# The affine maps of four layer norms moved from GpSimd to VectorE, in pieces between the stages that follow

## The chip, the cores and the metric

One Trainium2 chip; the kernel runs on 1 core. The metric is the time of one execution in microseconds (us). Engines are named as the profile names them: PE is TensorE's matmul stream, PEld its weight loads, DVE VectorE, ACT ScalarE, POOL GpSimd, SP the queue that issues most of the transfers. A line number such as L868 is a line of the kernel before.

## What is computed

The reference has two blocks of depth two on 512 tokens of width 1024 in 32-bit floats. The change lies in the second block, whose loop is:

```python
for l in range(DEPTH):
    mix = even_mixer(x, ...) if l % 2 == 0 else odd_mixer(x, ...)
    x = layer_norm(ALPHA * x + mix, ln1_g[l], ln1_b[l])
    hdn = jnp.square(jax.nn.relu(x @ ffn_w1[l]))
    x = layer_norm(ALPHA * x + hdn @ ffn_w2[l], ln2_g[l], ln2_b[l])
    e = rms_norm(p[l] @ ple_w_proj[l], ple_norm_g[l])
    x = x + jax.nn.sigmoid(x @ ple_w_gate[l]) * e
```

with `layer_norm(x, g, b) = (x - mean) * rsqrt(var + eps) * g + b`. So there are four layer norms, and each result is used twice: as the input of the next matrix product, and as the residual `x` to which that stage's result is added.

## The kernel before, in words

**Data.** The residual `x` lies in SBUF as 4 token tiles of 128 x 1024. Every matrix product runs at raised precision: each operand is split into a high part (rounded by a cast on ACT) and a low part (the rest, by a subtraction on DVE), and three matmuls go into the same PSUM tile (`mm3`, L140 to L142). A weight chunk of 512 KB is loaded by SP into `wraw` (3 buffers, L133), cast on ACT (`whi`, L134) and subtracted on DVE (`wlo`, L135). Activations are split in the same way (`Thi`, L291; `spt`, L293 or L295; `Tlo`, L296).

**Layer norm** (`layer_norm`, L844 to L861). For a pair of token tiles DVE computes the statistics (`bst` L854, `bmv` L855, `brs` L856 and L857), ACT the square root (L858), and DVE writes the normalised value over `x` (L859). PE transposes `x` (`psT`, L273), and the affine map for the matmul operand is applied after the transposition, when the tiles are split, with columns of gain and bias (L291 to L296). The residual needs the same map on `x` itself. That is `ln_affine`: POOL loads gain and bias as rows (`gr`, `br`, L821; one buffer each, used again by the next layer norm) and then, token tile by token tile, multiplies `x` by `gr` (L868) and adds `br` (L869), 128 x 1024 each. A tile's map can begin only when PE has transposed it.

**After ln1: the opening of the feed-forward stage.** `ple_e` (PE `pse`, ACT copies L920, squares L924, roots L927, DVE L925 to L928) is traced before it and runs beside ln1's second pair. Then `mlp` goes over 8 blocks of 512 hidden units. For a unit group `f`, `rows(f, o)` does 24 matmuls into `psu`, and then ACT takes the relu (`r`, L332), POOL squares it (`q`, L333), ACT rounds it (`uh`, L334) and DVE subtracts (`ul`, L335). In the first block, alone, the rows are cut in two halves of 256 tokens: f = 0, 1, 2 for the first half, f = 0, 1, 2 for the second, then f = 3 for both. After a block's rows come the matmuls with W2 into `psy`; the result is added to `x` on DVE (L877 the first time, L879 later), and that is where the mapped `x` is needed first.

**After ln2: the gate** (`ple_gate`). `proj_out` computes the gate's left 512 columns for the 4 token tiles (4 weight chunks, `psj`), then the right 512 columns (4 chunks with buffers of their own). Each result goes through `ev`: ACT takes the sigmoid (`pg`, L939), DVE multiplies by `e` (L940) and adds to `x` (L941). In layer 0 the next layer's activations are made from each finished tile (`pso`, L634; `Tlo`, L639); in layer 1 each finished tile is written out.

**Order.** Each engine works through its own queue in order. The queues are laid out when the kernel is built, from the order of the source and from when an instruction can start by an estimate; so an instruction that stands later in the source is put ahead where an earlier one isn't ready. `issue_after(i)` only adds that what is issued inside it stands behind `i` on `i`'s engine.

Of the kernel before, what the change touches and what calls it, by code (L numbers as in the profile page):

```python
# [18 lines left out]
P = 128  # L19
D = 1024  # L20
KT = D // P
# [57 lines left out]
def each(gen):  # L79
    return lambda t: next(gen, None)  # L80


def pairs(gen):
    return lambda t: t % 2 and next(gen, None)


class Net:
# [72 lines left out]

    def proj_out(self, acts, W, pp, rp, toks, evac, after, mid=None):
        hi, lo = acts
        self.proj_tok(acts, W[:, :512], pp, toks, lambda t, ps: evac(t, slice(0, 512), ps), mid)
        ps_of = lambda t: pp.tile([P, 512], F32, name="psj", tag="ps")[:, :256]
        if rp is None:
            for c0 in (512, 768):
                sl = slice(c0, c0 + 256)
                for t in self.proj_cols(acts, W[:, sl], ps_of, toks, lambda t, ps: evac(t, sl, ps)):  # L170
                    if c0 == 768:
                        after(t)
            return
        ws = [self.wsplit(W[c * 256:(c + 1) * 256, 512:].rearrange("(k p) n -> p k n", p=P), 2, 512, rp, f"w{c}") for c in range(KT // 2)]
        for t in toks:
            ps = pp.tile([P, 512], F32, name="psj", tag="ps")
            s = slice(t * P, (t + 1) * P)
            for k in range(KT):
                wh, wl = ws[k // 2]
                self.mm3(ps, hi[k][:, s], lo[k][:, s], wh[:, k % 2, :], wl[:, k % 2, :], k == 0, k == KT - 1)  # L180
            evac(t, slice(512, D), ps)
            after(t)
# [118 lines left out]

    def mlp(self, acts, W1, W2, T, st_name, add, ada=None, after=None):
        nc = self.nc
        hi, lo = acts
        toks = range(T // P)
        with ExitStack() as st:
            up = self.pool(st, st_name + "u", 2)
            tp = self.pool(st, st_name + "t", 2)  # L310
            by_pair = T <= 512
            lp = self.pool(st, st_name + "l", 1) if by_pair else None
            pu = self.pool(st, st_name + "pu", 3 if T > 512 else 2, PSUM)
            py = self.pool(st, st_name + "py", 2 if T > 512 else 4, PSUM)
            bg = iter(())
            if ada is not None:
                bg = self.ada_in(ada, (0,), self.pool(st, st_name + "pa", 1, PSUM), self.pool(st, st_name + "ra", 1))
            for fb in range(8):
                st_ = 256 if fb == 0 else 512
                us, ws = [], []  # L320
                for f in range(4):
                    us.append([up.tile([P, T], F32R, name="u" + n, tag=f"u{n}{f}") for n in "hl"])

                def rows(f, o):
                    w = min(st_, T - o)
                    (wh, wl), (uh, ul) = ws[f], us[f]
                    ps = pu.tile([P, 512], F32, name="psu", tag="psu")[:, :w]
                    for k in range(KT):
                        self.mm3(ps, wh[:, k, :], wl[:, k, :], hi[k][:, o:o + w], lo[k][:, o:o + w], k == 0, k == KT - 1)
                    r = tp.tile([P, 512], F32, name="r", tag="r")  # L330
                    q = tp.tile([P, 512], F32, name="q", tag="q")
                    nc.scalar.activation(r[:, :w], ps, AF.Relu)  # L332
                    nc.gpsimd.tensor_tensor(q[:, :w], r[:, :w], r[:, :w], MUL)  # L333
                    nc.scalar.copy(uh[:, o:o + w], q[:, :w])  # L334
                    nc.vector.tensor_tensor(ul[:, o:o + w], q[:, :w], uh[:, o:o + w].bitcast(F32), SUB)  # L335


                for fs in (range(3), range(3, 4)) if fb == 0 else ([f] for f in range(4)):
                    for f in fs:
                        fc = fb * 4 + f  # L340
                        ws.append(self.wsplit(W1[:, fc * P:(fc + 1) * P].rearrange("(k p) n -> p k n", p=P), KT, P))
                    for o in range(0, T, st_):
                        for f in fs:
                            rows(f, o)
                    for f in fs:
                        next(bg, None)
                last = fb == 7
                ws = {}
                for pr in ([toks[i:i + 2] for i in range(0, len(toks), 2)] if last and by_pair else [toks]):
                    for hf in range(2):  # L350
                        if hf not in ws:
                            ws[hf] = [self.wsplit(W2[(fb * 4 + 2 * c) * P:(fb * 4 + 2 * c + 2) * P, hf * 512:(hf + 1) * 512]
                                                  .rearrange("(k p) n -> p k n", p=P), 2, 512, *((lp, f"l{c}") if last and hf and by_pair else ())) for c in range(2)]

                        steps = [(t, range(4)) for t in pr]
                        if by_pair and hf == 0 and pr[0] == 0:
                            steps[:2] = [(t, fs) for fs in (range(3), range(3, 4)) for t in pr[:2]]
                        pss = {}
                        for t, fs in steps:
                            if t not in pss:  # L360
                                pss[t] = py.tile([P, 512], F32, name="psy", tag="psy")
                            ps, s = pss[t], slice(t * P, (t + 1) * P)
                            for f in fs:
                                wh, wl = ws[hf][f // 2]
                                self.mm3(ps, us[f][0][:, s], us[f][1][:, s], wh[:, f % 2, :], wl[:, f % 2, :], f == 0, f == 3)
                            if fs[-1] < 3:
                                continue
                            add(t, hf, ps, last)
                            if last and hf and after is not None:
                                after(t)  # L370
            for _ in bg:
                pass
# [445 lines left out]
class Net2(Net):  # L818
# [45 lines left out]
    def ln_affine(self, x, nm, layer, tp):  # L864
        gr = self.bcast_row(tp, self.A[nm + "_g_2"][layer], D, "gr")
        br = self.bcast_row(tp, self.A[nm + "_b_2"][layer], D, "br")
        for t in range(NX):
            self.nc.gpsimd.tensor_tensor(x[:, t, :], x[:, t, :], gr, MUL)  # L868
            self.nc.gpsimd.tensor_tensor(x[:, t, :], x[:, t, :], br, ADD)  # L869

    def res_add(self, x, first):
        nc = self.nc
# [16 lines left out]
            return f  # L889
        return first  # L890

    def ffn(self, x, acts, layer, after):
        self.mlp(acts, self.A["ffn_w1_2"][layer], self.A["ffn_w2_2"][layer], SX, f"f{layer}", self.res_add(x, self.firsts()), after=after)


    def ple_e(self, pool, layer):
# [31 lines left out]
                nc.vector.scalar_tensor_tensor(e[:, t, :], in0=e[:, t, :], scalar=ss, in1=gr, op0=MUL, op1=MUL)  # L928
        return e

    def ple_gate(self, x, acts, e, layer, after):
        nc, A = self.nc, self.A
        with ExitStack() as s:
            tp = self.pool(s, "plgt", 1)
            pp = self.pool(s, "plgps", 6, PSUM)

            def ev(t, c, ps):
                g = tp.tile([P, 512], F32, name="pg", tag="pg", bufs=3)
                nc.scalar.activation(g, ps, AF.Sigmoid)  # L939
                nc.vector.tensor_tensor(g, g, e[:, t, c], MUL)  # L940
                nc.vector.tensor_tensor(x[:, t, c], x[:, t, c], g, ADD)  # L941
            self.proj_out(acts, A["ple_w_gate_2"][layer], pp, tp, list(range(NX)), ev, after)


    def rope16(self, z, t, nh, cosp, sinp, tp):
# [443 lines left out]
    def second(self, x, acts, Tp, done):  # L1389
        with ExitStack() as s0:  # L1390
# [3 lines left out]
            for layer in range(2):  # L1394
# [14 lines left out]
                s = ExitStack()  # L1409
                ep = self.pool(s, "ep", 1)  # L1410
                e = self.ple_e(ep, layer)
                self.ln_affine(x, "ln1", layer, ep)
                nacts = self.act_tiles(Yp, SX)
                ln2 = self.layer_norm(x, "ln2", layer, nacts, lp)
                self.ffn(x, acts, layer, pairs(ln2))
                drain(ln2)
                self.ln_affine(x, "ln2", layer, ep)
                if layer == 0:
                    Xp = self.pool(s0, "U2", 1, side="right")
                    acts = self.act_tiles(Xp, SX)  # L1420
                    xa = self.x_acts(x, acts)
                    self.ple_gate(x, nacts, e, layer, each(xa))
                    drain(xa)
                else:
                    self.ple_gate(x, nacts, e, layer, done)
                s.close()
                self.dbg(f"l{layer}", x)

# [64 lines left out]
class Net3(Net2):  # L1493
# [832 lines left out]
    def first(self, st):  # L2326
        self.prologue()
        x, xc = self.layer0(self.rwkv_norm)
        self.dbg0(x, xc)
        return self.layer1(x, st)  # L2330
# [43 lines left out]
```

## Time and profile before

| | us |
|---|---|
| median of 3 runs | 3755.2 (3750.63 to 3758.21) |
| the profiled execution | 3759.0 |
| its span in the profile | 3757.2 |
| PE busy in it | 3554.0 |
| DVE busy | 2065.8 |
| ACT busy | 1531.4 |
| POOL busy | 726.0 |

The span is the part of the execution that the profile shows; 1.8 us lie around it. The four places of the change are called here by what they are: the opening of layer 0 (from about 2584 us of the span to 2645), the first gate (2955 to 3033), the opening of layer 1 (3296 to 3366) and the last gate (3681 to the end). A row with a bracket at its end gives the idle time of the engine before that instruction and what ended it. Busy times of engines overlap and don't add up to the span.

### The profile page before, as it was taken

How to read it: one execution, taken by the hardware profiler on the slowest of the kernel's cores; microseconds unless marked ns; L12 is line 12 of the kernel's file. 1: busy time of each engine (PE TensorE's matmuls, PEld its weight loads, DVE VectorE, ACT ScalarE, POOL GpSimd, SP SyncE). 2: the span in 40 equal slices, each digit the busy share in tenths (PEclk: the TensorE clock that was granted, in tenths of full speed). 3: DMA queues.
4: the chain of work that ended last, by engine and by line, in shares of the span. 5: the costliest groups of instructions: out<-in, count | busy, mean ns of one | idle time of the engine just before them, and what ended most of it. 6: DMA issues, size and time to landing. Idle time of an engine off the chain costs nothing.

```text
span 3757.2 us, 63564 instructions
## 1 busy us (share of the span) xinstructions
PE 3554.0 (95%) x26108; PEld 2920.4 (78%) x26108; DVE 2065.8 (55%) x3937; ACT 1531.4 (41%) x2956; POOL 726.0 (19%) x588
## 2 busy tenths in 40 slices
PE   7999999999989988889799999998999899989998
PEld 5767877888865657777588889988888799978886
DVE  5556433333457778899454345567444744573346
ACT  5556332222234655556442234354222345442233
POOL 2100033433222010001224440003111200031112
PEclk9999999999989998888899999999999999989999
DMA  5132233222222782322433332122333321223332
GB/s 182 61 103 95 68 99 104 64 65 62 73 88 71 277 298 91 92 80 87 157 118 95 96 95 91 57 63 87 103 97 90 96 64 60 78 79 100 97 95 68
DMA packets 308211, 370.80 MB, mean 99 GB/s; under 512 B 31712, under 2 KB 228304, under 8 KB 305872
## 3 DMA queue, kind: packets, MB, share of 16 engines
q1 hardware_dynamic: 298752, 340.28, 28.7%
q0 software_dynamic: 8912, 26.39, 2.2%
q8 instruction: 205, 3.36, 0.4%
q14 instruction: 86, 0.70, 0.1%
q10 hardware_dynamic: 256, 0.07, 0.0%
HBM read 324.71 MB, written 41.98 MB: 98 GB/s over the span
## 4 chain that ended last, share of the span: by engine, by line
PE 53%; DVE 9%; ACT 2%; issue 2%; DMA 1%; POOL 0%; SPq 0%; DVEq 0%; ACTq 0%; POOLq 0%
PE psu L142 5%; PE psu L141 5%; PE psu L140 5%; PE psy L142 5%; PE psy L140 4%; PE psy L141 4%; PE psj L140 4%; PE psj L142 4%; PE psj L141 4%; DVE T L2078 1%; DVE Tlo L296 1%; DVE pr L2077 1%; PE S L972 1%; PE psk L140 1%; PE psk L141 1%
## 5 line engine op out<-in xcount | busy, mean ns | idle before, releaser
L135 DVE TENSOR_TENSOR wlo<-wraw,whi 128x1024 fp32r<-128x1024 f32 (+1 forms) x402 | 505.3, 1259 | 543.1 <-ACT whi L134 542.4
L134 ACT CAST whi<-wraw 128x1024 fp32r<-128x1024 f32 (+1 forms) x402 | 417.1, 1039 | 920.2 <-PE psy L142 528.2
L140 PE MATMUL psu<-Thi,whi 128*128 128x512 f32 (+1 forms) x1408 | 499.9, 355 | 8.7 <-ACT r L332 6.0
L142 PE MATMUL psu<-Thi,wlo 128*128 128x512 f32 (+1 forms) x1408 | 501.1, 356 | 0.3 <-DVE wlo L135 0.3
L141 PE MATMUL psu<-Tlo,whi 128*128 128x512 f32 (+1 forms) x1408 | 499.6, 355 | 0.0
L140 PE MATMUL psj<-whi,Thi 128*128 128x256 f32 (+1 forms) x1568 | 482.9, 310 | 10.4 <-ACT whi L134 7.6
L142 PE MATMUL psj<-whi,Tlo 128*128 128x256 f32 (+1 forms) x1568 | 473.8, 303 | 2.5 <-DVE Tlo L296 2.5
L141 PE MATMUL psj<-wlo,Thi 128*128 128x256 f32 (+1 forms) x1568 | 474.3, 303 | 1.2 <-DVE wlo L135 1.0
L140 PE MATMUL psy<-whi,uh 128*128 128x512 f32 x1152 | 452.7, 393 | 3.3 <-ACT whi L134 2.0
L142 PE MATMUL psy<-whi,ul 128*128 128x512 f32 x1152 | 455.0, 395 | 0.0
L141 PE MATMUL psy<-wlo,uh 128*128 128x512 f32 x1152 | 452.3, 393 | 0.0
L333 POOL TENSOR_TENSOR q<-r 128x512 f32<-128x512 f32 (+1 forms) x176 | 235.3, 1337 | 880.0 <-ACT r L332 880.0
L140 PEld LDWEIGHTS psj<-whi,Thi 128*128 128x128 f32 x1568 | 300.2, 192 | 27.4 <-ACT whi L134 9.5
L142 PEld LDWEIGHTS psj<-whi,Tlo 128*128 128x128 f32 x1568 | 299.6, 191 | 15.0 <-DVE Tlo L296 4.2
L141 PEld LDWEIGHTS psj<-wlo,Thi 128*128 128x128 f32 x1568 | 300.3, 192 | 13.0 <-DVE wlo L135 2.5
L140 PEld LDWEIGHTS psu<-Thi,whi 128*128 128x128 f32 x1408 | 268.3, 191 | 52.1 <-ACT r L332 8.1
L141 PEld LDWEIGHTS psu<-Tlo,whi 128*128 128x128 f32 x1408 | 268.4, 191 | 40.7
L142 PEld LDWEIGHTS psu<-Thi,wlo 128*128 128x128 f32 x1408 | 268.3, 191 | 38.5 <-DVE wlo L135 0.7
L335 DVE TENSOR_TENSOR ul<-q,uh 128x512 fp32r<-128x512 f32 (+1 forms) x176 | 105.0, 597 | 316.4 <-ACT uh L334 316.1
L142 PEld LDWEIGHTS psy<-whi,ul 128*128 128x128 f32 x1152 | 216.8, 188 | 53.2 <-DVE ul L335 6.5
L140 PEld LDWEIGHTS psy<-whi,uh 128*128 128x128 f32 x1152 | 216.7, 188 | 52.3 <-ACT whi L134 2.4
L141 PEld LDWEIGHTS psy<-wlo,uh 128*128 128x128 f32 x1152 | 216.9, 188 | 47.2
(545 smaller groups left out, 6100.8 us busy)
## 6 DMA issues: line engine op xcount, KB each, us to landing
wraw<-in_mlp_w_dram SPq DMA_DIRECT2D x128, 512.0 KB, 3.9
wraw<-in_ffn_w_dram SPq DMA_DIRECT2D x128, 512.0 KB, 3.8
wraw<-in_ada_w_dram SPq DMA_DIRECT2D x64, 512.0 KB, 4.8
wraw<-in_ev_w_in_dram SPq DMA_DIRECT2D x28, 512.0 KB, 3.6
scr_bk<-BK SPq DMA_DIRECT2D x16, 768.0 KB, 3.3
wraw<-in_od_w_in_dram SPq DMA_DIRECT2D x24, 512.0 KB, 3.6
BK<-scr_bk SPq DMA_DIRECT2D x14, 768.0 KB, 4.7
wraw<-in_rwkv_w_rkv_dram SPq DMA_DIRECT2D x16, 512.0 KB, 4.6
```

The lines of the kernel that those rows point to most:

```text
L134: nc.scalar.copy(hi, raw)
L135: nc.vector.tensor_tensor(lo, raw, hi.bitcast(F32), SUB)
L140: mm(ps, lhsT=ah, rhs=bh, start=start, stop=False)
L141: mm(ps, lhsT=ah, rhs=bl, start=False, stop=False)
L142: mm(ps, lhsT=al, rhs=bh, start=False, stop=stop)
L296: nc.vector.tensor_tensor(lo[k][:, s], t[:, :w], hi[k][:, s].bitcast(F32), SUB)
L333: nc.gpsimd.tensor_tensor(q[:, :w], r[:, :w], r[:, :w], MUL)
L335: nc.vector.tensor_tensor(ul[:, o:o + w], q[:, :w], uh[:, o:o + w].bitcast(F32), SUB)
L972: nc.tensor.matmul(S[e][:, c], lhsT=q[r], rhs=k[r, c], start=True, stop=True)
L2077: nc.vector.tensor_tensor(pv, T[:, j + 1:, j:j + 1].to_broadcast([P, n, j]), T[:, j:j + 1, 0:j].to_broadcast([P, n, j]), MUL)
L2078: nc.vector.tensor_tensor(T[:, j + 1:, 0:j], T[:, j + 1:, 0:j], pv, ADD)
```

## The change

`ln_affine` still loads the rows `gr` and `br`, but no longer issues the map. It returns a function `affine(t, c)` that multiplies and adds on VectorE, for token tile `t` and columns `c`, behind the last VectorE instruction traced so far. In the feed-forward stage `affine(f)` for whole tiles is called after `rows(f, second half)` for f = 0, 1, 2 and after `rows(3, first half)`, in the first block only. In the gate, the left 512 columns of all four tiles are mapped after the left half's matmuls and before its first evaluation; the right 512 columns of tile 0 after the left half's last evaluation, and of tile t + 1 after the right half's evaluation of tile t. The splitting of the right half's weights (`last_ws`) now stands in the source ahead of the left half's evaluations and behind those four maps.

```diff
-    def proj_out(self, acts, W, pp, rp, toks, evac, after, mid=None):
+    def proj_out(self, acts, W, pp, rp, toks, evac, after, mid=None, between=None):
         hi, lo = acts
-        self.proj_tok(acts, W[:, :512], pp, toks, lambda t, ps: evac(t, slice(0, 512), ps), mid)
+        ws = []
+
+        def last_ws():
+            if rp is not None and not ws:
+                ws.extend(self.wsplit(W[c * 256:(c + 1) * 256, 512:].rearrange("(k p) n -> p k n", p=P), 2, 512, rp, f"w{c}") for c in range(KT // 2))
+
+        def first(t, ps):
+            if between is not None and t == toks[0]:
+                between()
+                last_ws()
+            evac(t, slice(0, 512), ps)
+        self.proj_tok(acts, W[:, :512], pp, toks, first, mid)
...
-        ws = [self.wsplit(W[c * 256:(c + 1) * 256, 512:].rearrange("(k p) n -> p k n", p=P), 2, 512, rp, f"w{c}") for c in range(KT // 2)]
+        last_ws()
...
                     for o in range(0, T, st_):
                         for f in fs:
                             rows(f, o)
+                            if early is not None and fb == 0 and (f == 3) != (o > 0):
+                                early(f)
...
     def ln_affine(self, x, nm, layer, tp):
         gr = self.bcast_row(tp, self.A[nm + "_g_2"][layer], D, "gr")
         br = self.bcast_row(tp, self.A[nm + "_b_2"][layer], D, "br")
-        for t in range(NX):
-            self.nc.gpsimd.tensor_tensor(x[:, t, :], x[:, t, :], gr, MUL)
-            self.nc.gpsimd.tensor_tensor(x[:, t, :], x[:, t, :], br, ADD)
+
+        def affine(t, c=slice(0, D)):
+            with self.tc.issue_after(self.last_of(mybir.EngineType.DVE)):
+                self.nc.vector.tensor_tensor(x[:, t, c], x[:, t, c], gr[:, c], MUL)
+                self.nc.vector.tensor_tensor(x[:, t, c], x[:, t, c], br[:, c], ADD)
+        return affine
+
+    def last_of(self, engine):
+        return next(i for i in reversed(self.nc.cur_bb.bb.instructions) if i.engine == engine)
...
                 nc.scalar.activation(g, ps, AF.Sigmoid)
                 nc.vector.tensor_tensor(g, g, e[:, t, c], MUL)
                 nc.vector.tensor_tensor(x[:, t, c], x[:, t, c], g, ADD)
-            self.proj_out(acts, A["ple_w_gate_2"][layer], pp, tp, list(range(NX)), ev, after)
+                n = t + 1 if c.start else t + 1 - NX
+                if 0 <= n < NX:
+                    affine(n, slice(512, D))
+
+            def mid():
+                for t in range(NX):
+                    affine(t, slice(0, 512))
+            self.proj_out(acts, A["ple_w_gate_2"][layer], pp, tp, list(range(NX)), ev, after, between=mid)
```

The remaining lines hand `affine` from `second` through `ffn` and `ple_gate`.

## Rows read from the trace of the kernel before

**Rows 1.** The page: busy us, share of the span and instructions of each engine.
```profile
PE 3554.0 (95%) x26108; PEld 2920.4 (78%) x26108; DVE 2065.8 (55%) x3937; ACT 1531.4 (41%) x2956; POOL 726.0 (19%) x588
```

**Rows 2.** Groups on POOL, whole span: count | busy us, mean ns | idle before, releaser.
```profile
L868 POOL TENSOR_TENSOR x<-x,gr 128x1024 f32<-128x1024 f32 x16 | 42.5, 2679 | 105.2 <-PE psT L273 102.2 <-DMA gr<-in_ln_g_dram 3.0
```

**Rows 3.** Timeline of POOL, first gate: start us, duration us, engine, line.
```profile
2963.23 5.07 POOL L868 TENSOR_TENSOR x<-x,gr 128x1024 f32<-128x1024 f32 x2 [16.95 <-PE psT L273]
```

**Rows 4.** Timeline of DVE, first gate, the same columns.
```profile
2963.41 2.63 DVE L296 TENSOR_TENSOR Tlo<-spt,Thi 128x256 fp32r<-128x256 f32 x1
...
2984.33 0.43 DVE L296 TENSOR_TENSOR Tlo<-spt,Thi 128x256 fp32r<-128x256 f32 x1
...
3009.38 1.21 DVE L135 TENSOR_TENSOR wlo<-wraw,whi 128x1024 fp32r<-128x1024 f32 x1
...
3010.52 0.68 DVE L940 TENSOR_TENSOR pg<-pg,ple_e 128x512 f32<-128x512 f32 x1
```

**Rows 5.** Groups on DVE, 2963 to 2974 (first gate, pair one on POOL).
```profile
L296 DVE TENSOR_TENSOR Tlo<-spt,Thi 128x256 fp32r<-128x256 f32 x4 | 8.9, 2235 | 0.0
```

**Rows 6.** Groups on DVE, 2586 to 2611 (opening of layer 0).
```profile
L296 DVE TENSOR_TENSOR Tlo<-spt,Thi 128x256 fp32r<-128x256 f32 x8 | 13.4, 1702 | 0.5 <-ACT spt L293 0.4
...
L135 DVE TENSOR_TENSOR wlo<-wraw,whi 128x1024 fp32r<-128x1024 f32 x3 | 5.7, 1894 | 0.0
```

**Rows 7.** Groups on DVE, 3302 to 3335 (opening of layer 1).
```profile
L296 DVE TENSOR_TENSOR Tlo<-spt,Thi 128x256 fp32r<-128x256 f32 x13 | 16.1, 1246 | 1.6 <-ACT spt L293 1.5
...
L135 DVE TENSOR_TENSOR wlo<-wraw,whi 128x1024 fp32r<-128x1024 f32 x3 | 5.9, 1953 | 0.0
```

**Rows 8.** Waits of PE, 2962 to 3003 (first gate): us in total, times, longest.
```profile
PE psT L273 <- DVE bmv L855: 8.2, 1, 8.2
...
PE psj L142 <- DVE Tlo L296: 1.3, 2, 0.8
```

**Rows 9.** Waits of PE, 2588 to 2615 (opening of layer 0).
```profile
PE pse L140 <- DVE pTl L911: 3.1, 1, 3.1
...
PE psu L140 <- ACT ple_e L920: 2.7, 1, 2.7
...
PE pse L140 <- ACT ple_e L920: 0.6, 1, 0.6
```

**Rows 10.** Waits of PE, 3302 to 3341 (opening of layer 1).
```profile
PE psT L273 <- DVE x L859: 5.0, 2, 2.9
...
PE pse L140 <- DVE pTl L911: 3.4, 1, 3.4
...
PE psu L140 <- ACT r L332: 3.2, 1, 3.2
...
PE pse L140 <- ACT ple_e L920: 1.2, 1, 1.2
```

**Rows 11.** PE in four stretches: length, busy (count), granted clock, DMA share, GB/s.
```profile
2614.00:2621.00 7.00, 6.89 (x34) 0.55 0.54 195
2979.00:2986.00 7.00, 6.32 (x20) 0.53 0.58 207
3340.00:3344.00 4.00, 4.00 (x21) 0.57 0.41 131
3705.50:3709.50 4.00, 3.66 (x14) 0.54 0.63 202
```

**Rows 12.** DVE in the opening of layer 0, the same columns.
```profile
2628.00:2644.00 16.00, 7.17 (x10) 1.00 0.44 131
```

**Rows 13.** Timeline of DVE there: [idle us <-releaser].
```profile
2628.89 0.42 DVE L335 TENSOR_TENSOR ul<-q,uh 128x256 fp32r<-128x256 f32 x1 [0.94 <-ACT uh L334]
```

**Rows 14.** PE there, matmuls on W2 alone (tile psy): length, busy (count), granted clock.
```profile
2637.00:2643.00 6.00, 5.91 (x26) 1.00 0.39 111
```

**Rows 15.** Timeline of POOL there.
```profile
2627.06 1.37 POOL L333 TENSOR_TENSOR q<-r 128x256 f32<-128x256 f32 x1 [3.03 <-ACT r L332]
...
2635.46 0.61 POOL L333 TENSOR_TENSOR q<-r 128x256 f32<-128x256 f32 x1 [0.80 <-ACT r L332]
```

More of the change, by code (lines that the diff above doesn't have):

```diff
@@ L300, in act_tiles, with mlp @@
         return tuple(Parts(pool.tile([P, KT, width or T], F32R, name="T" + n, tag=tag + n)[:, :, :T]) for n in ("hi", "lo"))
-    def mlp(self, acts, W1, W2, T, st_name, add, ada=None, after=None):
+    def mlp(self, acts, W1, W2, T, st_name, add, ada=None, after=None, early=None):
         nc = self.nc
@@ L890, in firsts, with ffn @@
         return first
-    def ffn(self, x, acts, layer, after):
-        self.mlp(acts, self.A["ffn_w1_2"][layer], self.A["ffn_w2_2"][layer], SX, f"f{layer}", self.res_add(x, self.firsts()), after=after)
+    def ffn(self, x, acts, layer, after, affine):
+        self.mlp(acts, self.A["ffn_w1_2"][layer], self.A["ffn_w2_2"][layer], SX, f"f{layer}", self.res_add(x, self.firsts()), after=after, early=affine)
     def ple_e(self, pool, layer):
@@ L929, in ple_e, with ple_gate @@
         return e
-    def ple_gate(self, x, acts, e, layer, after):
+    def ple_gate(self, x, acts, e, layer, after, affine):
         nc, A = self.nc, self.A
@@ L1411, in second @@
                 e = self.ple_e(ep, layer)
-                self.ln_affine(x, "ln1", layer, ep)
+                affine = self.ln_affine(x, "ln1", layer, ep)
                 nacts = self.act_tiles(Yp, SX)
                 ln2 = self.layer_norm(x, "ln2", layer, nacts, lp)
-                self.ffn(x, acts, layer, pairs(ln2))
+                self.ffn(x, acts, layer, pairs(ln2), affine)
                 drain(ln2)
-                self.ln_affine(x, "ln2", layer, ep)
+                affine = self.ln_affine(x, "ln2", layer, ep)
                 if layer == 0:
@@ L1421, in second @@
                     xa = self.x_acts(x, acts)
-                    self.ple_gate(x, nacts, e, layer, each(xa))
+                    self.ple_gate(x, nacts, e, layer, each(xa), affine)
                     drain(xa)
                 else:
-                    self.ple_gate(x, nacts, e, layer, done)
+                    self.ple_gate(x, nacts, e, layer, done, affine)
                 s.close()
```

## The prediction, made before the changed kernel was run

> **What bounds the kernel now.** I read the page first, then the groups of the lines that the change takes out, then the four places where they run: POOL's and DVE's timelines side by side, PE's waits there, and the granted clock behind the longest waits. PE is busy for 95% of the span [rows 1], so over the whole kernel it is the bound, and only time in which PE stands still, or runs at the lower clock because it stood still, can be won. The map's two lines hold POOL for 16 multiplications of 2.68 us [rows 2] and 16 additions of about the same, and no engine is shown waiting for their results. What matters is what they do to DVE. While POOL multiplies [rows 3], DVE's subtraction of one `Tlo` tile takes 2.63 us; the same shape takes 0.43 us when POOL is idle [rows 4]. The 2.63 ends when POOL's instruction of about 2.5 us (two in 5.07) ends: the two engines don't share the time, one stands until the other has finished. Subtractions of two SBUF tensors are hit in this way wherever a map runs.
>
> The Trainium skill says the same in SBUF — State Buffer, section "Who interferes with whom": a VectorE instruction with two SBUF inputs contends with a GpSimd instruction that reads SBUF, and whichever issues first holds the pair of ports for the whole instruction. The rows agree. By that rule the change turns the block around, which is the third rival below.
>
> How long DVE stood so: in the first gate, four `Tlo` took 8.9 us instead of 4 x 0.43, so 7.2 [rows 5]. In layer 0's opening eight took 13.4 (10.0 too much) and three `wlo` 5.7 instead of 3 x 1.21 (2.1) [rows 4, 6]. In layer 1's opening thirteen took 16.1 (10.5) and three `wlo` 5.9 (2.3) [rows 7]. PE's waits at the same places are for DVE, or for an ACT that waits in its queue for DVE: 8.2 and 1.3 in the first gate [rows 8]; 3.1, 2.7 and 0.6 in layer 0's opening [rows 9]; 5.0, 3.4, 3.2 and 1.2 in layer 1's [rows 10]. The last gate repeats the first within 0.1 us in each wait, so it is costed by the first gate's rows. Behind the waits PE ran at the lower of its two levels, 1.2 instead of 2.4 GHz, for most of each stretch: 0.55, 0.53, 0.57 and 0.54 granted [rows 11].
>
> **What goes.** The 32 POOL instructions. *First gate*: the 8.2 us wait is for the norm of the second pair, which stands in DVE's queue behind those four `Tlo`; without 7.2 it is 1.0. The 1.3 comes from the second pair's map, and goes. The stretch at 0.53 had 6.32 us busy [rows 11], of which 0.47, 3.0 us, was lost; a wait of 1.0 should not bring it. 7.2 + 1.3 + 3.0 = 11.5. *Last gate*: the same with a shorter low stretch, 3.66 x 0.46 = 1.7, so 10.2. *Layer 0's opening*: of the first 3.1 only 2.1 is the stretched `wlo` (the rest is the transposition of the second pair); 2.7 and 0.6 are for ACT, which waited for the roots behind DVE. 5.4, and 6.89 x 0.45 = 3.1 of clock: 8.5. *Layer 1's opening*: 12.8 of waits against 12.8 of stretching. I take 10 of it, since the norm's own steps keep part of the first two waits, and 4.00 x 0.43 = 1.7 of clock: 11.7. In all 41.9.
>
> **What comes.** A DVE subtraction of 128 x 1024 takes 1.21 us and a product of 128 x 512 in SBUF 0.68 [rows 4]; the maps are of these shapes and both inputs lie in SBUF. An opening gets 8 x 1.21 = 9.7 us, a gate 16 x 0.68 = 10.9, over both layers 41.2, about as much as goes. What of it lies on the path?
>
> In an opening they stand between `ul` of the second half, which begins at 2628.89 [rows 13], and the first additions to `x`. In 2628 to 2644 DVE is busy for 7.17 of 16 us [rows 12], so 8.8 is free for 9.7. Behind the maps in DVE's queue stand the four later `ul` and two `wlo` of W2's first chunks: from 2629.3, 9.7 + 4 x 0.43 + 2 x 1.21 ends at 2643.1. PE begins with W2 at 2637.1, 26 matmuls in 5.91 us, so 0.23 each [rows 14], and wants the second chunk after 6 of them, at 2638.5. It would be 4.6 late, against 18 matmuls (4.1 us) on the first chunk that the other three token tiles offer, if the queue of PE is laid out so. Bounds: 0, and 4.6 with 3.1 of low clock, 7.7. I take 2 for each opening, near the low end, because that cover is almost as long as the delay. POOL's queue loses its only long work; the next `gr` and `br` loads, which reuse the buffers, wait there for the last map, and a `q` behind them for up to one map (2.4 us), beside rows that PE has already done. SP's queue keeps its order; the right half's weight loads are moved ahead of the evaluations in the source only.
>
> In a gate the left maps (8 x 0.68 = 5.4) lie where DVE, rid of the stretching, has room; they can stand ahead of a `Tlo` or a `wlo` one at a time. The right maps stand behind an evaluation each and ahead of the next, where PE needs 24 matmuls of 0.23, 5.5 us, for a tile and DVE 4 x 0.68 = 2.7; in layer 0 they can hold up a `Tlo` of the next layer by 1.4, which that pace hides. The last evaluation has no map behind it, so the tail is as before. Bounds 0 and 5.4; I take 1 for each gate, one or two maps, as only one at a time can slip in.
>
> **The sum.** 41.9 - 2 x 2 - 2 x 1 = 35.9 less. Against the profiled execution, 3759.0, that is 3723.1; the median of the runs shown is 3.8 lower, and for it I predict 3755.2 - 35.9 = 3719.
>
> **Rivals.** *DVE is overfilled in the openings.* The split of W2's second chunk comes late and PE doesn't fill the time: 7.7 instead of 2, twice, 11.4 worse: 3731. For it: 9.7 into 8.8 free. Against: the order is laid out with the maps in it.
>
> *The waits were hidden work anyway.* With DVE faster, ACT's casts or the weight loads end PE's waits in half of the places: 20.9 - 6 = 15 less, 3740. For it: two of layer 0's three waits name ACT. Against: in all four places the stretched DVE operations are as long as the waits.
>
> *The block turned around.* POOL's square `q` takes 1.37 us beside a DVE subtraction and 0.61 alone [rows 15]. Behind a pair of maps it would wait for up to 2.4, and `uh`, `ul` and the matmuls with W2 with it: 2.4 and 3.1 of clock for each opening, 11 worse: 3730. This is the other half of the rule cited from the Trainium skill's page SBUF — State Buffer. It decides if the four `q` between the maps are late in a row.
>
> *Slower than before.* DVE becomes the bound: all 41.2 us of maps lie on the path where PE's 41.9 went, and the waits, cut into pieces, bring back about 3 of low clock in each of four places: 12 - 0.7, 11 slower, 3766. It decides from DVE being full from the first map to the last evaluation; the 7.17 of 16 speaks against it.
>
> *It doesn't do what it says.* `issue_after` binds only from one side, so maps may be laid late, just ahead of the additions to `x`; PE then waits there as long as it did before: 3755.
>
> **How the numbers follow.** Forecast 0.54; overfilled openings 0.14; hidden waits 0.12; the block turned around 0.12; no change 0.04; slower 0.04. The range starts where all of the 12.8 and of the 3.1 goes (3.8 more) and no map costs anything: 3755.2 - 45.7 = 3709.5, less a little for the spread of the runs, 3708. It ends where both openings and both gates cost their upper bounds, 41.9 - 15.4 - 10.8 = 15.7 less, 3740, which takes in the first three rivals; with the spread 3742. About 0.2% (7.5 us) is what a measurement of this kernel can tell from no change. Faster by more 0.92, within it 0.04, slower by more 0.04.
>
> **What would show it.** In the changed profile: no `Tlo` of 128 x 256 over 0.5 us in the gates; the 8.2 us waits near 1, with the clock at its higher level behind them; no wait of ACT's roots over 2 us in the openings; maps at 1.2 and 0.68 us on DVE; and W2's first matmuls without a wait over 1 us. The prediction is wrong if the openings show a wait of PE for `wlo` of W2 or for `ul`, if waits for ACT take the place of those for DVE, or if the gates keep a wait over 3 us.

## The result and the profile after

The changed kernel takes 3708.3 us in the median of 4 runs (3706.4 to 3711.9), the kernel before beside it 3754.3: a ratio of 0.9878, 95% interval 0.9863 to 0.9894, or 46 us less. 35.9 were forecast. The profiled execution took 3707.4 us and has a span of 3705.6.

The engines' line of its page:

```profile
PE 3531.0 (95%) x26108; PEld 2905.1 (78%) x26108; DVE 2047.2 (55%) x3985; ACT 1530.7 (41%) x2956; POOL 639.3 (17%) x556
```

DVE took over 48 instructions and is busy for 18.6 us less than in [rows 1]: 42.3 us of maps came, and 60.9 of its other work went, most of it standing beside POOL. The maps on DVE, and what became of the subtractions of [rows 5], as groups of DVE (the whole span; for `Tlo` the first gate, 2950 to 3010 of this span):

```profile
L885 DVE TENSOR_TENSOR x<-x,br 128x512 f32<-128x512 f32 x16 | 11.0, 688 | 0.3
L884 DVE TENSOR_TENSOR x<-x,gr 128x512 f32<-128x512 f32 x16 | 10.9, 684 | 0.0
L885 DVE TENSOR_TENSOR x<-x,br 128x1024 f32<-128x1024 f32 x8 | 10.7, 1340 | 0.1
L884 DVE TENSOR_TENSOR x<-x,gr 128x1024 f32<-128x1024 f32 x8 | 9.7, 1213 | 0.0
```

```profile
L308 DVE TENSOR_TENSOR Tlo<-spt,Thi 128x256 fp32r<-128x256 f32 x9 | 3.7, 421 | 0.3 <-ACT spt L305 0.3
```

The 42.3 compare with 41.2 in the forecast; only the additions of the openings are longer than the rows had it (1.34 for 1.21), since `q` on POOL now holds them at times. A `Tlo` takes 0.42 where [rows 5] had 2.24 in the mean.

PE's waits at the four places, first gate (2950 to 2985), layer 0's opening (2570 to 2640) and layer 1's (3265 to 3320), against [rows 8 to 10]:

```profile
PE psT L285 <- DVE bmv L869: 0.9, 1, 0.9
PE psj L140 <- ACT Thi L303: 0.2, 1, 0.2
```

```profile
PE psT L285 <- DVE bmv L869: 3.7, 1, 3.7
PE pse L140 <- DVE pTl L932: 1.0, 1, 1.0
```

```profile
PE psT L285 <- ACT spt L305: 2.0, 2, 1.3
PE pse L140 <- DVE pTl L932: 1.6, 1, 1.6
PE psT L285 <- DVE x L873: 1.2, 2, 0.7
PE pse L140 <- ACT ple_e L941: 0.5, 1, 0.5
```

In the gate 8.2 became 0.9, and the 1.3 for `Tlo` is gone; 0.2 for ACT is left. In layer 0's opening 1.0 of 6.4 is left; the 3.7 comes from ahead of the map's place and is the same before (2586.44 of that trace, also 3.7). In layer 1's opening the 2.0 for ACT's `spt` and 0.5 of the 1.2 for `x` are in the kernel before as well, ahead of the window of [rows 10] or not shown in it (1.3 and 0.7; 0.6). So 2.8 of 12.8 is left. PE in stretches behind those places (length, busy, granted clock), first after:

```profile
3657.00:3663.00 6.00, 5.72 (x30) 1.00 0.61 180
2955.00:2961.00 6.00, 4.92 (x24) 1.00 0.56 180
2605.00:2640.00 35.00, 35.00 (x218) 1.00 0.45 135
3300.00:3340.00 40.00, 40.00 (x246) 1.00 0.41 119
2578.00:2588.00 10.00, 7.49 (x24) 0.50 0.79 238
3277.50:3284.50 7.00, 6.29 (x19) 0.51 0.21 59
```

Then two of the trace before:

```profile
2586.50:2596.50 10.00, 6.84 (x22) 0.50 0.64 181
3303.00:3320.00 17.00, 8.79 (x24) 0.50 0.13 35
```

The four low stretches of [rows 11], at the lower clock level, are gone, and in the two openings PE works without a pause at the higher level from ahead of the first map to behind the last. Two low stretches that [rows 11] doesn't show are still there. The one in layer 0's opening, behind the 3.7 us wait that stays, is as long as before. The one in layer 1's opening is 7 us long where the kernel before had 17.

**Where the time went, place by place.** Each instruction of PE and ACT was looked up in both traces, and the difference of its starts taken; the median of these differences is flat between the four places and steps at each. The steps, in us (minus is earlier), for all kernels of this study against the trace before:

| kernel | opening 0 | gate 1 | opening 1 | gate 2 | sum | median of runs |
|---|---|---|---|---|---|---|
| forecast, net | -6.5 | -10.5 | -9.7 | -9.2 | -35.9 | 3719 |
| changed kernel | -9.4 | -11.2 | -13.6 | -10.5 | -44.7 | 3708.3 |
| e1_openings | -10.3 | 0.0 | -14.5 | 0.2 | -24.6 | 3728.1 |
| e2_gates | -1.9 | -10.9 | -0.2 | -10.3 | -23.4 | 3734.6 |
| e3_dve_old_place | -8.7 | -10.9 | -7.0 | -10.4 | -37.0 | 3719.1 |
| e4_pool_new_place | 2.5 | -5.0 | -6.3 | -4.3 | -13.0 | 3742.9 |
| e5_no_map | -9.0 | -11.3 | -15.4 | -10.1 | -45.8 | 3708.4 |
| e6_weights_late | -9.7 | -11.3 | -13.2 | -10.0 | -44.2 | 3711.6 |
| e7_pool_write_only | -5.7 | -10.8 | -14.8 | -9.7 | -41.1 | 3716.2 |
| e8_double_map | -1.4 | -11.4 | -3.8 | -10.4 | -27.1 | 3729.6 |

The part ahead of the first place, which no kernel here changes, is itself up to 8.7 us shorter than in the trace before, so spans alone can't be compared to better than that; the steps can, to about 2 us (e2 shows 1.9 where it changes nothing). Each step is read from one execution of each kernel.

The last four runs (e5 to e8) were timed in another series than the first four, and the kernel before took 3749.4 in it and 3754.1 in the first. Each ratio below is to the kernel before of its own series.

### The profile page after: what moved, and what is told of

Same layout as the page of the kernel before. It is cut to its first block, busy times and chain, and to the rows that moved or that the text cites. A ratio compares the mean times of both kernels' runs of the same rounds, so it can differ in the third digit from the quotient of the medians.

```text
span 3705.6 us, 63555 instructions
## 1 busy us (share of the span) xinstructions
PE 3531.0 (95%) x26108; PEld 2905.1 (78%) x26108; DVE 2047.2 (55%) x3985; ACT 1530.7 (41%) x2956; POOL 639.3 (17%) x556
## 4 chain that ended last, share of the span: by engine, by line
PE 81%; DVE 11%; ACT 3%; DMA 3%; issue 2%; POOL 0%; SPq 0%; ACTq 0%; DVEq 0%; POOLq 0%
PE psy L142 7%; PE psu L142 7%; PE psu L141 7%; PE psu L140 7%; PE psy L140 7%; PE psy L141 7%; PE psj L140 6%; PE psj L142 6%; PE psj L141 6%; PE po L593 2%; DVE T L2107 1%; PE psk L140 1%; DVE pr L2106 1%; PE S L549 1%; PE pst L568 1%
## 5 line engine op out<-in xcount | busy, mean ns | idle before, releaser
L135 DVE TENSOR_TENSOR wlo<-wraw,whi 128x1024 fp32r<-128x1024 f32 (+1 forms) x402 | 493.1, 1229 | 538.1 <-ACT whi L134 537.3
L142 PEld LDWEIGHTS psj<-whi,Tlo 128*128 128x128 f32 x1568 | 299.2, 191 | 10.8 <-DVE Tlo L2323 0.4
```

The source lines that it names most:

```text
L135: nc.vector.tensor_tensor(lo, raw, hi.bitcast(F32), SUB)
L142: mm(ps, lhsT=al, rhs=bh, start=False, stop=stop)
```

## The experiments

The theory: POOL's maps held DVE's operations on two SBUF tensors, DVE's queue held PE, and each of the four places gave back its own waits. The rivals: the place in the source and not the engine made the gain; the earlier weights made a part of it; the moved work has a price that the gain hides.

**One half at a time.** e1_openings moves only ln1's maps:

```diff
     def ln_affine(...):
+        if nm == "ln2":
+            for t in range(NX):
+                self.nc.gpsimd.tensor_tensor(x[:, t, :], x[:, t, :], gr, MUL)
+                self.nc.gpsimd.tensor_tensor(x[:, t, :], x[:, t, :], br, ADD)
+            return lambda *a: None
...
-            self.proj_out(..., ev, after, between=mid)
+            self.proj_out(..., ev, after)
```

> Only the two maps after ln1 (the openings) are moved; the gates are as before the change. Theory (the gain is the end of VectorE's stretching by GpSimd, place by place): the traces of before and after shift against each other by 9.4 us in layer 0's opening and 13.6 in layer 1's, so about 23 less than before, near 3731, and the first gate keeps a wait of 8.2 us. Rival (the stages lean on each other, for instance through the order of the queues): the sum differs from 23 by more than 5.

Measured: 3728.1, ratio 0.9937 (0.9922 to 0.9951). The steps are 10.3 and 14.5 in the openings and none in the gates, where the waits of [rows 8] stand as they did:

```profile
PE psT L285 <- DVE bmv L869: 8.2, 1, 8.2
PE psj L142 <- DVE Tlo L308: 1.2, 2, 0.8
```

e2_gates has the same lines with `nm == "ln1"`, and keeps `between=mid`.

> Only the two maps after ln2 (the gates) are moved; the openings are as before. Theory: 11.2 and 10.4 us, so about 21.6 less than before, near 3733. Together with the run on the openings the two gains make up the whole of 46. Rival (stages lean on each other): differs from 21.6 by more than 5.

Measured: 3734.6, ratio 0.9951 (0.9936 to 0.9966). Steps of 10.9 and 10.3 in the gates; layer 1's opening keeps its waits of 5.0, 3.3, 3.2 and 1.2. The medians of the two halves fall by 26.0 and 19.6, together 45.6 of 46: the places don't lean on each other.

**Engine or place.** e3_dve_old_place issues the maps on DVE where POOL's were, in a plain loop, and drops `between=mid`, so the right half's weights stand where they stood before:

```diff
-        def affine(t, c=slice(0, D)):
-            with self.tc.issue_after(self.last_of(mybir.EngineType.DVE)):
...
+        for t in range(NX):
+            self.nc.vector.tensor_tensor(x[:, t, :], x[:, t, :], gr, MUL)
+            self.nc.vector.tensor_tensor(x[:, t, :], x[:, t, :], br, ADD)
+        return lambda *a: None
```

> The maps are on VectorE but at the place in the source where GpSimd's were, whole tiles, without the order behind a VectorE instruction; the right half's weights as before. Theory (the engine makes the gain, the place saves a part): no VectorE operation is stretched, so at least half of the 46 us is kept, 3715 to 3735, with maps standing ahead of splits. Rival (the place makes the gain, VectorE would be the bound without it): within 8 us of before, 3746 to 3762.

Measured: 3719.1, ratio 0.9912 (0.9896 to 0.9929), 35 of 46 us. In three places the step is the changed kernel's within 0.7; in layer 1's opening it is 7.0 instead of 13.6, most of it for one wait of PE (3265 to 3320):

```profile
PE psu L142 <- DVE wlo L135: 5.3, 1, 5.3
```

All eight instructions of the map stand there on DVE ahead of the split of the first W1 chunk, which runs from 3299.47 to 3300.69; PE goes on at 3300.74. In layer 0's opening that split had been done before the maps. So the engine makes most of the gain, and the place matters where a split of weights that PE wants next stands behind the maps.

e4_pool_new_place keeps the new places and goes back to POOL:

```diff
-            with self.tc.issue_after(self.last_of(mybir.EngineType.DVE)):
-                self.nc.vector.tensor_tensor(x[:, t, c], x[:, t, c], gr[:, c], MUL)
-                self.nc.vector.tensor_tensor(x[:, t, c], x[:, t, c], br[:, c], ADD)
+            with self.tc.issue_after(self.last_of(mybir.EngineType.Pool)):
+                self.nc.gpsimd.tensor_tensor(x[:, t, c], x[:, t, c], gr[:, c], MUL)
+                self.nc.gpsimd.tensor_tensor(x[:, t, c], x[:, t, c], br[:, c], ADD)
```

> The maps are at the new places but on GpSimd. Theory (the engine makes the gain): GpSimd's maps stretch VectorE's operations there, and in the openings a map of about 5 us per tile stands ahead of the square q that comes every 3.1 us, so most of the gain is lost: 3735 to 3765. Rival (moving the maps away from the layer norms makes the gain): 3708 to 3715.

Measured: 3742.9, ratio 0.9972 (0.9963 to 0.9982), 11 of 46 us. POOL's timeline in layer 0's opening, and DVE's groups in the first gate (2945 to 3005):

```profile
2615.79 2.41 POOL L884 TENSOR_TENSOR x<-x,gr 128x1024 f32<-128x1024 f32 x1
2618.27 2.47 POOL L885 TENSOR_TENSOR x<-x,br 128x1024 f32<-128x1024 f32 x1
2620.70 1.59 POOL L345 TENSOR_TENSOR q<-r 128x256 f32<-128x256 f32 x1
2622.25 2.35 POOL L884 TENSOR_TENSOR x<-x,gr 128x1024 f32<-128x1024 f32 x1
```

```profile
L135 DVE TENSOR_TENSOR wlo<-wraw,whi 128x1024 fp32r<-128x1024 f32 x10 | 16.7, 1682 | 0.7 <-ACT whi L134 0.6
L308 DVE TENSOR_TENSOR Tlo<-spt,Thi 128x256 fp32r<-128x256 f32 x16 | 14.8, 940 | 0.1
```

A `q` comes behind each pair of maps, and PE waits 2.7 for `uh`, 2.2 for `r` and 1.4 for `ul` there; in the gate a `Tlo` still takes 0.94 in the mean. Place alone is not it.

**What the moved work costs.** e5_no_map leaves the map of the residual out: `ln_affine` returns a function that does nothing, so gain and bias are not applied to `x`.

> The four affine maps of the residual are left out altogether, so this is the changed kernel without the work that was moved. Theory (at its new place the map is covered almost entirely): within 4 us of the changed kernel's 3708. Rival (the forecast's charge of 6 us for VectorE in the openings and gates is real, or larger): 3702 or less.

Measured: 3708.4, ratio 0.9885 (0.9861 to 0.991). That is the changed kernel's time, but the two come from different series, and the intervals of the ratios would leave room for 6 us. The steps decide: 45.8 without the maps against 44.7 with them, and only layer 1's opening differs, by 1.8. That is below what the steps can tell, and it lies elsewhere: the low stretch of that opening is shorter in this execution, 3.5 us for 7, and in the changed kernel it ends 25 us ahead of the first map (3309.57). The line of e5_no_map:

```profile
3278.00:3281.50 3.50, 3.00 (x12) 0.53 0.00 0
```

Behind the first map PE stood in neither opening of the changed kernel (the two lines at 1.00 above), and in the first gate it waited 0.2 us twice. So no cost of the maps can be shown, and the rival's 6 us fall.

e8_double_map adds `br` three times instead of once, so that the added work doubles (and the residual is another one).

> In the changed kernel each map is one multiplication and three additions instead of one, so VectorE's added work doubles from 41 to 82 us (the result is another one). Theory (the openings are nearly full, 8.8 us free for 9.7; the gates have some room): 5 to 9 us more in each opening and 1 to 5 in each gate, 3720 to 3736. Rival (VectorE's work at these places is far from the path): under 5 us in all, 3713 or less.

Measured: 3729.6, ratio 0.9937 (0.9917 to 0.9958). The openings lose 8.0 and 9.8 of their steps, the gates nothing: 11.4 and 10.4 stand. In each opening PE has one long wait, here layer 0's (2600 to 2665):

```profile
PE psy L141 <- DVE wlo L135: 6.9, 1, 6.9
```

So the openings were just full, as 9.7 for 8.8 free had it, while the gates still have room for another 11 us. The total came as expected, its parts not quite: the second opening loses more than the 5 to 9, and the gates nothing instead of 1 to 5.

**The weights.** e6_weights_late drops the one line `last_ws()` behind `between()`, so the right half's weights stand behind the evaluations again.

> The changed kernel with the splitting of the gate's right-half weights standing in the source behind the left half's evaluations, as before the change. Theory (they start when their buffers come free, wherever they stand): within 3 us of 3708. Rival (a part of the gates' 21.6 us comes from this move): 3712 or more, with a wait of TensorE for wlo in the gates.

Measured: 3711.6, ratio 0.989 (0.9871 to 0.9909). The median lies between the two, 0.6 outside the theory's 3 us and 0.4 short of the rival. But the gates' steps are the changed kernel's within 0.5, 11.3 and 10.0, and PE's waits in the first gate are 0.9 and 0.2 again, none for `wlo`. The profiled execution takes 4.7 us longer than the changed kernel's, and 4.3 of it lie ahead of the first place. That move does nothing that can be told here.

**What of POOL holds DVE.** e7_pool_write_only puts, in the kernel before's place, a product of one column and five fills with zeros for each token tile; the maps are left out, and `between=mid` with them.

```diff
+        for t in range(NX):
+            i = self.nc.gpsimd.tensor_tensor(x[:, t, :1], x[:, t, :1], gr[:, :1], MUL).ins
+            with self.tc.issue_after(i):
+                for _ in range(5):
+                    self.nc.gpsimd.memset(br, 0.0)
+        return lambda *a: None
```

> At the place of the maps before the change GpSimd multiplies one column of the tile (to wait for the transposition as the map did) and then fills a 128x1024 tile with zeros five times; the maps themselves are left out. Theory (VectorE is held by GpSimd's reading of SBUF, as the Trainium skill's SBUF page has it): Tlo of 128x256 stays at 0.43 us beside the fills, and the time is near 3705 to 3720. Rival (any GpSimd instruction holds VectorE): Tlo beside a fill takes about a fill longer, 1 us or more, and the time is 3728 or more.

Measured: 3716.2, ratio 0.9899 (0.9877 to 0.9921). Timelines of POOL and of DVE in the first gate:

```profile
2966.09 2.39 POOL L886 MEMSET br<- 128x1024 f32 x2
2968.45 0.49 POOL L883 TENSOR_TENSOR x<-x,gr 128x1 f32<-128x1 f32 x1
2968.88 1.96 POOL L886 MEMSET br<- 128x1024 f32 x2
```

```profile
2964.62 0.82 DVE L873 TENSOR_SCALAR x<-x,bmv,brs 128x1024 f32<-128x1024 f32 x1
...
2966.20 1.38 DVE L873 TENSOR_SCALAR x<-x,bmv,brs 128x1024 f32<-128x1024 f32 x1 [0.27 <-ACT brs L872]
2967.66 1.23 DVE L135 TENSOR_TENSOR wlo<-wraw,whi 128x1024 fp32r<-128x1024 f32 x1
2968.89 0.54 DVE L307 TENSOR_SCALAR spt<-psT,n2col 128x256 f32<-128x256 f32 x1
2969.47 0.42 DVE L308 TENSOR_TENSOR Tlo<-spt,Thi 128x256 fp32r<-128x256 f32 x1
```

Beside the fills the subtractions take 1.23 and 0.42, which is what they take alone (1.21 and 0.43 in [rows 4]); the longest `Tlo` of this run takes 0.45. One operation is longer: the normalisation of 128 x 1024, one SBUF tensor and two scalars, 1.38 beside a fill and 0.82 without. That is the distinction that the Trainium skill makes in SBUF — State Buffer, section "Who interferes with whom": two SBUF inputs contend with a GpSimd instruction that reads SBUF and not with one that only writes it, while an operation in a two-port mode contends with either. For the subtractions the trace agrees. For the normalisation it agrees if that runs in such a mode, which no run here shows by itself.

The step of layer 0's opening is smaller, 5.7. Four fills and the next load of `br` stand in POOL's queue between the first squares `q` there; PE waits 1.9 for `r` (2604 to 2640), and 9 us from 2619 on have a granted clock of 0.81.

None of the runs points to a version that would beat the changed kernel: without any map no gain can be told, and in the stages of the change no subtraction of a `Tlo` is held any more.

## Why the prediction was right, and where its sizes were off

**The cause** was right and is shown from both sides. With the maps on DVE the stretching goes, and the gain comes at the old place too, in full in three of four (e3); with the maps on POOL most of it is lost at the new places too (e4). The two halves add up (e1, e2).

**The signs given beforehand** came as named: `Tlo` at 0.42, the 8.2 at 0.9 with the clock at its higher level behind it, no wait of PE for `wlo` or `ul` in the openings, none over 1 us for W2's first matmuls, maps at 1.21 and 0.68 (an opening's additions at 1.34).

**The gain before costs** was forecast as 41.9; without the maps it is 45.8. Gates: 11.5 and 10.2 forecast, 11.3 and 10.1 measured. Layer 0's opening: 8.5 and 9.0. Layer 1's opening was sized too small, 11.7 for 15.4. The waits themselves were right there, 10 of 12.8 forecast and 10.0 gone in the changed kernel. What was left out is the earlier low stretch of that opening. The kernel before runs 8.79 us of matmuls in it at 0.50, so it loses half of them, 4.4; after it is 6.29 at 0.51, 3.1, and in e5_no_map 3.00 at 0.53, 1.4. That adds 1.3, or 3.0 in e5, to the forecast's 1.7 of clock behind the last wait. 10.0, 1.3 and 1.7 make 13.0 of the changed kernel's 13.6.

The count of the standing was short as well. It has only operations on two SBUF tensors, but the normalisation, with one, was held beside the maps too, in both openings. In layer 1's (0.81 us without a map, the same columns as [rows 4]):

```profile
3308.26 2.38 DVE L859 TENSOR_SCALAR x<-x,bmv,brs 128x1024 f32<-128x1024 f32 x1
```

PE's first wait for `x` there, 2.1 us of the 5.0 in [rows 10], ends with this operation; in the changed kernel it is gone, and 0.7 of the second is left.

**The costs** were the weak term: 2 for each opening and 1 for each gate, 6 in all; the runs show 45.8 - 44.7 = 1.1, which can't be told from nothing. In the gates the maps fill DVE's pauses, and even twice as many do (e8). In the openings the reckoning of how full DVE is was right, since doubling them brings the wait that the first rival described, 6.9 us for the second W2 chunk; with the maps once, the layout of DVE's queue puts that split between the two halves of a map:

```profile
2616.71 0.83 DVE L347 TENSOR_TENSOR ul<-q,uh 128x256 fp32r<-128x256 f32 x1
2617.46 1.21 DVE L884 TENSOR_TENSOR x<-x,gr 128x1024 f32<-128x1024 f32 x1
2618.60 1.21 DVE L135 TENSOR_TENSOR wlo<-wraw,whi 128x1024 fp32r<-128x1024 f32 x1
2619.73 1.63 DVE L885 TENSOR_TENSOR x<-x,br 128x1024 f32<-128x1024 f32 x1
```

The prediction had set it behind all four maps, at 2643 of the old span. It is done at 2619.81, PE begins with W2 at 2620.73, and PE is busy for 35 of 35 us around it.

**The rivals.** *Overfilled openings*: not at this size, but real at double. *Waits hidden by ACT*: fell, the waits for ACT's copies went with DVE's. *The block turned around*: it is there and small. `q` takes 0.65 to 1.71 beside the maps and a map's addition 1.34 instead of 1.21, and nobody on PE waits for it. *Slower* and *no change* fell.

With 3708.3 the median lies at the low end of the range (3708), which had been set from all of the 12.8 and of the 3.1 going and from no cost. The second came, the first didn't: 2.8 and 1.0 of those waits are left. The shorter low stretch, which the sum didn't have, and differences that the steps can't tell made up for it. That the time still fell inside the range is in part luck. The sizes erred in one direction: costs counted though their cover was named, and a low-clock stretch not counted though layer 1's first waits were seen.

## What to carry to other kernels

An engine that nobody waits for can still be on the path: look for the same operation and shape with two durations in one queue, and for what runs beside the long ones. Where GpSimd's two-input work overlaps VectorE's subtractions, moving it to VectorE can be free, though VectorE is the busier of the two (55% against 17% here), if it is laid in pieces where the queue has pauses and not ahead of a split that TensorE wants next. Count the clock behind every wait that goes, and not only behind the longest.

## What the runs showed of the hardware that was not expected

A fill on POOL (0.95 us for 128 x 1024) leaves a DVE subtraction of two SBUF tensors at 0.42 and 1.23 us but lengthens a one-tensor normalisation from 0.82 to 1.38; a map on POOL lengthens that normalisation to 2.38. And the time of one unchanged part, the 2560 us ahead of the first place, differs by up to 8.7 us between the profiled executions of these kernels on a single core, more than several of the effects measured here; steps between aligned traces resolved them where whole times could not.
